# A fused two-layer decoder on one core: constants spread out, the layer change reordered, second-layer steps moved

## The chip, the cores and the metric

The kernel runs on one core of a Trainium2 chip. The core has a matrix engine (TensorE, PE in the profile), a vector engine (VectorE, DVE), a scalar engine (ScalarE, ACT), a general one (GpSimd, POOL) and a queue that only issues transfers (SyncE, SP). ACT and POOL issue transfers too. Engines run their own instructions in order and wait for one another by semaphores. TensorE writes its results to PSUM banks of 128 x 512 numbers; everything else lives in SBUF tiles, or in the chip's main memory (DRAM in the code).

The metric is the device time in microseconds (us) of one execution; lower is better.

## The reference

The input is 512 tokens of 2048 channels, float32, and two residual layers are applied, each `x <- x + W_out(mixer(RMSNorm(x)) * silu(gate))`:

```python
def reference(x, positions, ...):
    hn = rms_norm(x, norm_w[0])                      # layer 0: differential attention, 8 heads
    q, k, v, gate = split(hn @ da_w_in)              # 2048 x 8192
    a = softmax(q1 k1) - lam * softmax(q2 k2)        # causal, RMS-normed and rotated q, k
    x = x + (rms_norm(a @ v) * silu(gate)) @ da_w_out
    hn = rms_norm(x, norm_w[1])                      # layer 1: RWKV-7, 32 heads of 64
    p = token_shift_mix(hn @ rw_w_in, mu)            # r, k, v, gate and two low-rank inputs
    # per head, per token: S = S * w + (S a) b + v k ;  y = S r
    y = group_norm(wkv7_scan(r, w, k, v, -kk, kk * a)) + bonus
    return x + (y * silu(g)) @ rw_w_out
```

The recurrence over tokens is what makes layer 1 more than projections: each head keeps a 64 x 64 state that every token changes.

## The kernel before, in words

Each float32 operand of a large product is split into a high part (a rounded copy, by ACT) and a low part (the rest, by DVE), and three products stand for one (`mm3`). Weights are loaded by SP as `wraw` and split into `wh` and `wl` (`split_w`, L102 and L103), two tiles of each in turn. All large products are recorded under L114.

The order of the work is made in two ways. The instructions are traced in program order, and a planner then orders each engine's instructions by priority as its own estimates of their durations make them ready; `high_priority` with the offsets AHEAD, SCAN and SOLVE (2000, 3000, 4000) lifts a block. Second, a `Chain` is a generator whose pieces of side work are put between matmuls: every matmul of the first `mm3` that carries `g` counts as a tick (`tick`), only the oldest chain counts, and when its wait has run out the next piece is traced, its PE instructions behind that matmul (`issue_after`). The number that a piece yields is the wait to the next. `finish` runs the rest of a chain at once.

**Layer 0.** Per head, two units of 192 matmuls: queries and keys, then values and gate. The attention of head h-1 and the turning of head h's keys run as chains in them. Behind head 0, `rwkv_consts` loads the constants of layer 1 on SP, transposes them on PE (`load_rows`, L187) and derives small tiles on DVE. After the last head, the output projection takes rows that `split_rows` loads back from DRAM and splits (L415, L416); its second half of the columns is done with seven products instead of eight on blocks (`seven`), with sums of row blocks (`sum_forms`, loads `frow`) and of weight blocks.

**Layer change.** The last of the seven products go to the banks `z`. The sums of squares of x are then turned into scales, tokens 0 to 255 first and tokens 256 to 511 after the last product; DVE multiplies x by them (L760), PE transposes it (`xT`, L780), and the low-rank projection (`lora`) begins.

**Layer 1.** Channels go in 16 pairs of heads (j). For each pair there are projections of 48 matmuls: values V(j), keys K(j+1), gate G(j-3) from j = 3 on, receptances R(j+1), in this order. At matmul 18 of V(j) the callback `behind` finishes the chain of pair j-2, computes the Gram matrices of pair j (`gram`, L1004, results `gp`), steps the chain of pair j-1 if it is there, and starts `t_solve` of pair j: a triangular solve on DVE in 31 steps, whose inputs and result T go through DRAM (`ltd`, `LT`, `td`).

The chain of pair j is made at the top of the loop of j+1, and its first step is traced there: four loads of T into `TT` (L1081) and two transpositions on DVE (L1089). After GAP_D ticks the first products with T follow (`px`, L1095), with copies to `X`; after 19 more the second products (L1105) with copies into `TT`; after 8 more the scan, 8 chunks of three steps each (`sm`, L1176, L1187, L1194), with waits of 6, 6 and 8 ticks (4, 4 and 5 for pairs 1 and 14, 3, 3 and 4 for pair 0, whose count is lengthened by 28). Then come the outputs `Y` and `centre` (reductions `s`, L1231 to L1233). `group_norm` (`ysq`, `var`, `rsg`, `yc`) and `finish_y` (four transpositions of `yc`, L1254) end a pair. `px` has one PSUM bank, shared with the values' transpositions, `finish_y` and the sum of `stage_v` that `y` (L1119) reads.

After the loop stand G(13), G(14) and G(15). The chain of pair 15 is put in front of them with a wait of 66 ticks. Between G(14) and G(15) pair 14 is finished. Then rows 0 to 13 are loaded with SP and split, and the output projection follows as in layer 0: two plain column blocks, the second with the sums' loads on POOL's queue, then `seven`. Row 15 comes in the last part of the first column block (`all_rows`). The accumulators `acc` of `seven` use three tiles with the tag AR; the weight loader of `seven` uses tiles with the tags wraw, G1 and LT.

Of the kernel before, what the change touches and what calls it, by code (L numbers as in the profile page):

```python
# [23 lines left out]
P = 128  # L24
# [154 lines left out]

def load_rows(g, pieces, rows, queue=None):  # L180

    nc = g.nc
    t = g.tmpc.tile([P, P], F32, name="prow", tag="junk", bufs=2)
    for r0, n, ap in pieces:
        (queue or nc.sync).dma_start(out=t[r0 : r0 + n, :], in_=ap)
    ps = g.ps.tile([P, 512], F32, name="prp", tag="pc")
    nc.tensor.transpose(ps[:, :rows], t[:rows, :], g.ident[:rows, :rows])  # L187
    o = g.const.tile([P, rows], F32, name=f"prm{pieces[0][2].tensor.name}")
    g.made_prm = nc.vector.tensor_copy(o[:], ps[:, :rows]).ins
    return o  # L190
# [117 lines left out]
def head_vg(g, h, vg):  # L308

    nc, w = g.nc, g.work  # L310
    V = w.tile([P, NT, 256], F32R, name="V", tag="V", bufs=1)
    VL = w.tile([P, NT, 256], F32R, name="VL", tag="VL", bufs=1)
    G = w.tile([P, NT, 256], F32, name="G", tag="G", bufs=1)
    for t in range(NT):
        nc.scalar.activation(V[:, t, :], vg[t][:, 0:256], AF.Copy, scale=g.rstd0[:, t : t + 1])
        nc.vector.scalar_tensor_tensor(VL[:, t, :], vg[t][:, 0:256], g.rstd0[:, t : t + 1], V[:, t, :].bitcast(F32),
                                       ALU.mult, ALU.subtract)
        th = w.tile([P, 256], F32, name="th", tag="th", bufs=2)
        nc.scalar.activation(th[:], vg[t][:, 256:512], AF.Tanh, scale=g.hrstd0[:, t : t + 1])
        gs = w.tile([P, 256], F32, name="gs", tag="gs", bufs=2)  # L320
        nc.vector.scalar_tensor_tensor(gs[:], vg[t][:, 256:512], g.rstd0[:, t : t + 1], g.subw[:],
                                       ALU.mult, ALU.mult)
        nc.vector.scalar_tensor_tensor(G[:, t, :], th[:], 1.0, gs[:], ALU.add, ALU.mult)
    return V, VL, G
# [258 lines left out]
def layer0(g, aps):  # L583
# [86 lines left out]
    with ExitStack() as cx:  # L670
# [186 lines left out]
def rwkv_consts(g, aps):  # L857
# [24 lines left out]
    for nm, first, second in (("bk_s0", "hkk", "hka"), ("bk_b0", "hkk", "omka"),  # L882
# [3 lines left out]
        nc.vector.tensor_copy(o[C:], g.prm[second][C:])  # L886
        g.prm[nm] = o


# [181 lines left out]

GAP_D, GAP_X, GAP_T = 22, 19, 8

# [185 lines left out]
def layer1(g, aps):  # L1259
    nc, tc = g.nc, g.tc  # L1260
    with ExitStack() as cx:
# [97 lines left out]
        acc = {}  # L1359
        for nm in ("11", "22", "12", "21"):  # L1360
            t, c = PLACES[nm]
# [67 lines left out]
```

## Time and profile before

| | us |
|---|---|
| median of 3 runs | 2218.23 |
| lowest, highest | 2218.01, 2223.02 |
| profiled execution | 2227.16 |
| its span, first to last instruction | 2225.5 |
| TensorE busy in it | 2174.8 (98%) |
| VectorE, ScalarE, GpSimd busy | 1425.9, 1041.6, 337.9 |
| TensorE's mean granted clock | 0.994 |

A busy matrix engine is not one at its peak, since matmuls are pipelined. What counts is where it stood still, for what, and where its granted clock was below 1. In rows of waits stand the waiting engine, its result and line, then the one that released it; total in us, number of times, longest. In rows of groups or of the timeline, `out<-in` names the tiles. In the rows of stretches come the stretch, its length, the busy time of each engine with the number of its instructions, the granted clock, and the transfers' share and rate.

### The profile page before, as it was taken

What the parts mean: (1) busy time and instruction counts of PE and PEld (TensorE: products, weight loads), DVE (VectorE), ACT (ScalarE), POOL (GpSimd) and SP (SyncE); (2) the same over time, 40 slices, a digit from 0 to 9 for tenths busy, and PEclk for the clock granted to TensorE, in tenths of its full rate; (3) what the DMA queues carried; (4) which work ended last, traced back from release to release, by engine and by line L of the source; (5) the groups of instructions that cost most, each with busy time, mean ns of one, the idle gap of its engine ahead of it and who ended that gap; (6) DMA issues with size and microseconds to landing.
All of it is one profiled execution on the core that took longest, in us unless ns stands there. A gap on an engine that the chain in (4) does not pass through costs nothing. (4 is left out here: it accounts for less than half of the span.)

```text
span 2225.5 us, 33949 instructions
## 1 busy us (share of the span) xinstructions
PE 2174.8 (98%) x12202; PEld 1761.6 (79%) x12202; DVE 1425.9 (64%) x3772; ACT 1041.6 (47%) x2110; POOL 337.9 (15%) x724
## 2 busy tenths in 40 slices
PE   9999999999999999989999999999999999999999
PEld 7788888888888878867777777877777777777777
DVE  5664636455564676465677787776777877766545
ACT  6443434344343453335455555555555555544322
POOL 0000000000000000110333223323332222331101
PEclk9999999999999999999999999999999999999999
DMA  6223232222222455643423233333333333345465
GB/s 190 91 82 104 76 104 87 92 95 80 95 86 95 141 187 202 158 99 89 106 67 81 75 91 90 79 93 96 90 91 81 90 89 83 102 117 187 151 193 114
DMA packets 281421, 240.21 MB, mean 108 GB/s; under 512 B 31764, under 2 KB 239780, under 8 KB 281252
## 3 DMA queue, kind: packets, MB, share of 16 engines
q1 hardware_dynamic: 257220, 190.22, 29.2%
q0 software_dynamic: 15168, 31.81, 6.8%
q10 hardware_dynamic: 8864, 16.01, 2.0%
q8 instruction: 96, 1.57, 0.3%
q14 instruction: 73, 0.60, 0.1%
HBM read 217.98 MB, written 19.99 MB: 107 GB/s over the span
## 5 line engine op out<-in xcount | busy, mean ns | idle before, releaser
L103 DVE TENSOR_TENSOR wl<-wraw,wh 128x1024 fp32r<-128x1024 f32 (+2 forms) x319 | 388.2, 1217 | 439.7 <-ACT wh L102 431.8
L102 ACT CAST wh<-wraw 128x1024 fp32r<-128x1024 f32 (+2 forms) x319 | 333.5, 1046 | 481.5 <-PE pp L114 342.3
L114 PE MATMUL pp<-wh,hH 128*128 128x512 f32 x1268 | 500.0, 394 | 3.5 <-ACT hH L801 1.5
L114 PE MATMUL pp<-wl,hH 128*128 128x512 f32 x1268 | 496.9, 392 | 1.8 <-DVE wl L103 1.8
L114 PE MATMUL pp<-wh,hL 128*128 128x512 f32 x1268 | 497.9, 393 | 0.0
L114 PE MATMUL pp<-hH,wl 128*128 128x512 f32 x1024 | 416.1, 406 | 0.0
L114 PE MATMUL pp<-hH,wh 128*128 128x512 f32 x1024 | 414.8, 405 | 0.0
L114 PE MATMUL pp<-hL,wh 128*128 128x512 f32 x1024 | 414.3, 405 | 0.0
L114 PEld LDWEIGHTS pp<-wh,hH 128*128 128x128 f32 x1268 | 238.3, 188 | 52.5 <-ACT hH L801 1.8
L114 PEld LDWEIGHTS pp<-wl,hH 128*128 128x128 f32 x1268 | 238.3, 188 | 49.0 <-DVE wl L103 2.5
L114 PEld LDWEIGHTS pp<-wh,hL 128*128 128x128 f32 x1268 | 238.3, 188 | 48.0
L114 PEld LDWEIGHTS pp<-hH,wh 128*128 128x128 f32 x1024 | 194.4, 190 | 34.9 <-issue 1.7
L114 PEld LDWEIGHTS pp<-hL,wh 128*128 128x128 f32 x1024 | 194.3, 190 | 34.9 <-issue 0.2
L114 PEld LDWEIGHTS pp<-hH,wl 128*128 128x128 f32 x1024 | 194.4, 190 | 34.0
L450 POOL DMA_DIRECT2D frow<-yd x12 | 9.0, 748 | 888.0 <-DVE rs_i L63 737.2
L1065 DVE SCALAR_TENSOR_TENSOR tmpl<-LT,Tm 128x60 f32<-128x60 f32 (+24 forms) x496 | 133.7, 270 | 9.9
L1182 POOL COPY SA<-VS 64x64 f32<-64x64 f32 x224 | 55.6, 248 | 504.7 <-DVE VS L1198 424.5
L1067 DVE TENSOR_TENSOR Tm<-Tm,tmpl 128x60 f32<-128x60 f32 (+24 forms) x496 | 104.3, 210 | 11.5
L1179 ACT COPY rhs<-sm 64x64 f32<-64x64 f32 x256 | 52.8, 206 | 88.8 <-PE sm L1176 85.7
L1011 ACT COPY G<-gp 128x512 f32<-128x512 f32 x64 | 35.0, 591 | 90.2 <-PE gp L1004 89.9
L1189 ACT COPY VS<-sm 64x64 f32<-64x64 f32 x256 | 52.6, 206 | 39.9 <-PE sm L1187 35.3
L1187 PEld LDWEIGHTS sm<-rhs,TT 128*128 128x128 f32 x256 | 45.2, 189 | 26.4 <-ACT rhs L1179 18.4
(317 smaller groups left out, 3243.3 us busy)
## 6 DMA issues: line engine op xcount, KB each, us to landing
wraw<-in_rw_w_in_dram SPq DMA_DIRECT2D x128, 512.0 KB, 4.0
wraw<-in_da_w_in_dram SPq DMA_DIRECT2D x254, 256.0 KB, 3.0
wraw<-in_da_w_out_dram SPq DMA_DIRECT2D x26, 512.0 KB, 4.2
wraw<-in_rw_w_out_dram SPq DMA_DIRECT2D x26, 512.0 KB, 4.1
LT<-ltd POOLq DMA_DIRECT2D x64, 132.0 KB, 2.9
yr<-yd SPq DMA_DIRECT2D x28, 256.0 KB, 4.6
frow<-yd POOLq DMA_DIRECT2D x12, 512.0 KB, 5.8
xq<-in_x_dram SPq DMA_DIRECT2D x16, 256.0 KB, 5.5
```

The costliest lines, as they stand in the source:

```text
L102: nc.scalar.copy(hi[:, ks], raw[:, ks])
L103: nc.vector.tensor_sub(lo[:, ks], raw[:, ks], hi[:, ks].bitcast(F32))
L114: m = nc.tensor.matmul(out, a, b, start=s, stop=e, skip_group_check=skip)
L450: nc.gpsimd.dma_start(out=r, in_=src[k0 * P : (k0 + KG) * P, :].rearrange("(k p) t -> p k t", p=P))
L1011: nc.scalar.copy(p.G[:, c0 : c0 + 4, :, h, :], gp[h][:].rearrange("p (u x t) -> p u x t", u=4, x=2))
L1065: nc.vector.scalar_tensor_tensor(tt, LT[:, i : i + 1, i + 1 :].to_broadcast([P, s, n]), n2[:, i : i + 1], Tm[:, 0:s, i : i + 1].to_broadca ...
L1067: nc.vector.tensor_add(Tm[:, 0:s, i + 1 :], Tm[:, 0:s, i + 1 :], tt)
L1179: nc.scalar.copy(rhs[r_, :], sm[r_, h * C : h * C + C])
L1182: nc.gpsimd.tensor_copy(p.SA[r_, c - 1, :], VS[r_, c, h, :])
L1187: nc.tensor.matmul(sm[:, P : P + C], both(g.TT[j % 2][:, c]), rhs[:], start=True, stop=True)
L1189: nc.scalar.copy(VS[r_, c, h, :], sm[r_, P : P + C])
```

## The change

- `load_rows` is divided: `fetch_rows` loads, `load_rows` transposes and copies. `rwkv_consts` becomes a generator. Its loads go to POOL's queue instead of SP's, and its three transpositions and the derived constants become steps of a chain in the first unit of head 1, with waits of 10, 8, 8 and 8 ticks. The PSUM tag of the transpositions is another one. The attention of head 0, which comes behind this chain, waits 24 ticks after it instead of 40.
- `head_vg` keeps its last gate instructions on ACT and DVE; in layer 0, the splits of rows 8 to 13 are put behind them on these engines.
- At the layer change, the scales of tokens 0 to 255 lose the priority SOLVE; those of tokens 256 to 511 keep it.
- GAP_D is 18 instead of 22.
- Pair 14's transpositions, gating and split move from before G(15) to behind its 24th matmul; its gate is computed before them.
- Layer 1's rows are loaded into eight tags instead of four.
- The second and third sums of layer 1 load their rows into G1 tiles instead of LT and BK.
- The accumulators of layer 1 are allocated in the order 11, 21, 22, 12 instead of 11, 22, 12, 21.

```diff
+def fetch_rows(g, pieces, queue, tag="junk", bufs=2):
+    t = g.tmpc.tile([P, P], F32, name="prow", tag=tag, bufs=bufs)
     for r0, n, ap in pieces:
-        (queue or nc.sync).dma_start(out=t[r0 : r0 + n, :], in_=ap)
-    ps = g.ps.tile([P, 512], F32, name="prp", tag="pc")
+        queue.dma_start(out=t[r0 : r0 + n, :], in_=ap)
+    return t
+def load_rows(g, pieces, rows, queue=None, t=None):
+    t = t or fetch_rows(g, pieces, queue)
+    ps = g.ps.tile([P, 512], F32, name="prp", tag="pa", bufs=2)
...
+    g.gated = ta.ins, gd.ins
...
-def split_rows(g, src, tags, bufs, n=KT):
+def split_rows(g, src, tags, bufs, n=KT, late=KT, behind=()):
...
-        out.append(split_row(g, yr[:]))
+        with ExitStack() as after:
+            for ins in behind if k >= late else ():
+                after.enter_context(g.tc.issue_after(ins))
+            out.append(split_row(g, yr[:]))
...
-                Chain(g, attention(g, h - 1, *before, 40 if h < NH - 1 else 36), 40 if h < NH - 1 else 24)
+                Chain(g, attention(g, h - 1, *before, 40 if h < NH - 1 else 36), 40 if 1 < h < NH - 1 else 24)
...
-                rwkv_consts(g, aps)
-        rows = split_rows(g, g.yd, ("t1",), 4, KT - 2)
+                Chain(g, rwkv_consts(g, aps))
+                g.chains[0].step(g)
+        rows = split_rows(g, g.yd, ("t1",), 4, KT - 2, 8, g.gated)
...
-        with tc.high_priority(offset=SOLVE):
-            for half in (slice(0, 2), slice(2, 4)):
+        for half in (slice(0, 2), slice(2, 4)):
+            with tc.high_priority(offset=SOLVE if half.start else 0):
...
-    pb = load_rows(g, [(16 * i, 16, r16(r)) for i, r in enumerate(rows)], 112)
-    g.mu = load_rows(g, [(0, 64, r16(aps["rw_mu"][0, 0 : 4 * D]))], 64)
-    t = g.tmpc.tile([2, RK], F32, name="mut", tag="junk", bufs=2)
-    nc.sync.dma_start(out=t[:], in_=aps["rw_mu"][0, 4 * D :].rearrange("(j p) -> j p", p=RK))
-    ps = g.ps.tile([P, 512], F32, name="pt", tag="pc")
+    tb, tm = [fetch_rows(g, x, nc.gpsimd, "a") for x in (pbs, mus_)]
+    t = g.tmpc.tile([2, RK], F32, name="mut", tag="y", bufs=2)
+    nc.gpsimd.dma_start(out=t[:], in_=aps["rw_mu"][0, 4 * D :].rearrange("(j p) -> j p", p=RK))
+    yield 10
+    pb = load_rows(g, pbs, 112, t=tb)
+    yield 8
+    g.mu = load_rows(g, mus_, 64, t=tm)
+    yield 8
+    ps = g.ps.tile([P, 512], F32, name="pt", tag="pa", bufs=2)
...
+    yield 8
...
-GAP_D, GAP_X, GAP_T = 22, 19, 8
+GAP_D, GAP_X, GAP_T = 18, 19, 8
...
-        finish_y(g, j - 1, pairs[j - 1])
-        row = gated(g, j - 1, pairs[j - 1], gate(g, j - 1, gps), True)
-        gt = gate(g, j, proj(3, j))
-        rows = split_rows(g, g.yd2, ("r", "k", "th0", "th1"), 1, j - 1) + [row]
+        gt = gate(g, j - 1, gps)
+        row = []
+        def last_but_one(m):
+            with tc.issue_after(m.ins):
+                finish_y(g, j - 1, pairs[j - 1])
+                row.append(gated(g, j - 1, pairs[j - 1], gt, True))
+        gt = gate(g, j, proj(3, j, behind=(24, last_but_one)))
+        rows = split_rows(g, g.yd2, ("r", "k", "th0", "th1", "l", "f", "xH", "xL"), 1, j - 1) + row
...
-                frow = [w.tile([P, KG, 512], F32, name="frow", tag=t, bufs=1)[:] for t in ("LT", "BK")]
+                if sums:
+                    both = w.tile([P, 2, KG, 512], F32, name="frow", tag="G1", bufs=2)
+                    frow = [both[:, i] for i in range(2)]
+                else:
+                    frow = [w.tile([P, KG, 512], F32, name="frow", tag=t, bufs=1)[:] for t in ("LT", "BK")]
...
-        for nm in ("11", "22", "12", "21"):
+        for nm in ("11", "21", "22", "12"):
```

More of the change, by code (lines that the diff above doesn't have):

```diff
@@ L177, in unit_tok @@
     return pts
-def load_rows(g, pieces, rows, queue=None):
+def fetch_rows(g, pieces, queue, tag="junk", bufs=2):
+    t = g.tmpc.tile([P, P], F32, name="prow", tag=tag, bufs=bufs)
+    for r0, n, ap in pieces:
+        queue.dma_start(out=t[r0 : r0 + n, :], in_=ap)
+    return t
+def load_rows(g, pieces, rows, queue=None, t=None):
     nc = g.nc
-    t = g.tmpc.tile([P, P], F32, name="prow", tag="junk", bufs=2)
-    for r0, n, ap in pieces:
-        (queue or nc.sync).dma_start(out=t[r0 : r0 + n, :], in_=ap)
-    ps = g.ps.tile([P, 512], F32, name="prp", tag="pc")
+    t = t or fetch_rows(g, pieces, queue)
+    ps = g.ps.tile([P, 512], F32, name="prp", tag="pa", bufs=2)
     nc.tensor.transpose(ps[:, :rows], t[:rows, :], g.ident[:rows, :rows])
@@ L318, in head_vg @@
         th = w.tile([P, 256], F32, name="th", tag="th", bufs=2)
-        nc.scalar.activation(th[:], vg[t][:, 256:512], AF.Tanh, scale=g.hrstd0[:, t : t + 1])
+        ta = nc.scalar.activation(th[:], vg[t][:, 256:512], AF.Tanh, scale=g.hrstd0[:, t : t + 1])
         gs = w.tile([P, 256], F32, name="gs", tag="gs", bufs=2)
@@ L322, in head_vg @@
                                        ALU.mult, ALU.mult)
-        nc.vector.scalar_tensor_tensor(G[:, t, :], th[:], 1.0, gs[:], ALU.add, ALU.mult)
+        gd = nc.vector.scalar_tensor_tensor(G[:, t, :], th[:], 1.0, gs[:], ALU.add, ALU.mult)
+    g.gated = ta.ins, gd.ins
     return V, VL, G
@@ L861, in rwkv_consts @@
             aps["rw_r_k"][0].rearrange("h n -> (h n)"), aps["rw_gn_w"][0], aps["rw_gn_b"][0]]
-    pb = load_rows(g, [(16 * i, 16, r16(r)) for i, r in enumerate(rows)], 112)
-    g.mu = load_rows(g, [(0, 64, r16(aps["rw_mu"][0, 0 : 4 * D]))], 64)
-    t = g.tmpc.tile([2, RK], F32, name="mut", tag="junk", bufs=2)
-    nc.sync.dma_start(out=t[:], in_=aps["rw_mu"][0, 4 * D :].rearrange("(j p) -> j p", p=RK))
-    ps = g.ps.tile([P, 512], F32, name="pt", tag="pc")
+    pbs = [(16 * i, 16, r16(r)) for i, r in enumerate(rows)]
+    mus_ = [(0, 64, r16(aps["rw_mu"][0, 0 : 4 * D]))]
+    tb, tm = [fetch_rows(g, x, nc.gpsimd, "a") for x in (pbs, mus_)]
[7 more added lines that the diff above has]
+    ps = g.ps.tile([P, 512], F32, name="pt", tag="pa", bufs=2)
     nc.tensor.transpose(ps[:RK, :2], t[:], g.ident[:2, :2])
```

## The prediction

> **What bounds the kernel.** I read the page first, then the waits of TensorE (PE), then the clock by stage, then the timeline around the steps that the diff touches.
>
> ```profile
> span 2225.5 us, 33949 instructions
> PE 2174.8 (98%) x12202; PEld 1761.6 (79%) x12202; DVE 1425.9 (64%) x3772; ACT 1041.6 (47%) x2110; POOL 337.9 (15%) x724
> ```
>
> PE is the bound: no edit removes a matmul, so only PE's pauses, and matmuls that run slowly, can be won. The pauses by cause, and what plain products cost back to back in the chain of waits (the last row: start, duration, 19 products, so 0.228 us each):
>
> ```profile
> engine line waited for: us in total, times, longest us
> PE sm L1194 <- ACT VS L1189: 4.3, 15, 1.4
> PE xT L780 <- DVE xq L760: 4.0, 1, 4.0
> PE z L114 <- DVE wl L103: 3.7, 2, 3.4
> PE gp L1004 <- DVE s L1232: 3.2, 8, 0.7
> PE px L1095 <- DVE y L1119: 2.9, 1, 2.9
> PE px L1095 <- DVE T L1089: 2.4, 2, 1.5
> PE pt L1254 <- DVE yc L1247: 2.1, 2, 1.9
> PE pp L114 <- DVE wl L103: 1.8, 2, 1.1
> PE pt L114 <- DVE wl L103: 1.2, 1, 1.2
> PE pp L114 <- ACT hH L415: 0.9, 1, 0.9
> PE pp L114 <- DVE gs L321: 0.7, 1, 0.7
> PE pt L364 <- DVE a L358: 0.7, 1, 0.7
> PE prp L187 <- DVE prmin_rw_w_dram L189: 0.4, 1, 0.4
> PE pp L114 <- DVE prmin_rw_mu_dram L189: 0.3, 1, 0.3
> 1276.27 4.33 PE pp L114 x19
> ```
>
> Some pauses cost twice, because the clock drops behind them:
>
> ```profile
> core 0: us, PE busy (x) PEld busy (x) DVE busy (x) ACT busy (x) POOL busy (x), PEclk, DMA share, GB/s
> 979.00:983.00 4.00, 0.64 (x3) 0.54 (x4) 4.00 (x8) 0.39 (x1) 0.24 (x1) 0.99 0.00 0
> 983.00:986.40 3.40, 3.40 (x10) 2.47 (x9) 0.86 (x2) 0.00 (x0) 0.00 (x0) 0.50 0.41 116
> 1105.80:1109.20 3.40, 1.49 (x34) 1.41 (x35) 1.79 (x4) 1.03 (x2) 3.09 (x5) 1.00 0.92 231
> 1109.20:1116.00 6.80, 6.80 (x47) 5.24 (x46) 1.62 (x3) 3.42 (x7) 0.00 (x0) 0.50 0.13 39
> 2020.60:2024.00 3.40, 1.54 (x10) 1.04 (x9) 1.94 (x5) 1.63 (x2) 0.00 (x0) 1.00 0.55 122
> 2024.00:2027.40 3.40, 3.40 (x10) 2.62 (x9) 2.71 (x4) 0.63 (x1) 0.00 (x0) 0.50 0.32 102
> ```
>
> Each pair of rows is a stretch in which PE did little and the one behind it, at a granted clock of 0.50: 3.4 us at half speed is 1.7 us lost.
>
> **Layer change.** DVE scales the first half of x (eight operations) ahead of a weight split, because the block has priority SOLVE and the split only AHEAD:
>
> ```profile
> 976.01 5.16 DVE L760 TENSOR_SCALAR xq<-xq,rs 128x512 f32<-128x512 f32 x8
> 981.10 1.21 DVE L103 TENSOR_TENSOR wl<-T,wh 128x1024 fp32r<-128x1024 f32 x1
> ```
>
> PE's last products (z) wait 3.4 us for that split. At normal priority the split goes first; the scales follow while the products run. PE then has ten products and DVE only the second split (the ten products of 983.0 to 986.4 needed 0.86 us of DVE), so the scales fit ahead of the transpositions. What is late next is the second half's wait (xT, 4.0 us), which stays. With z's pause the half-speed stretch 983.0 to 986.4 should go. Gain 3.4 + 1.7 = 5.1; if the scales come late after all, 0.
>
> **Last gate.** The transpositions of pair 14 (L1254) stand between two gate projections and wait 1.9 us for its group norm. Moved 24 matmuls into the last projection (24 x 0.228 = 5.5 us), they come after the norm is done. The half-speed stretch 2024.0 to 2027.4 follows that pause: gain 1.9 + 1.7 = 3.6. Row 14 is needed only near the end of the next unit's 192 products.
>
> [...]
>
> **T's products.** GAP_D counts matmuls from the end of the previous chain. Now the scan chain, from the first products on, is 19 + 8 + 7 x (6+6+8) + 6+6 = 179 matmuls, and from matmul 18 of one value projection to the next there are 30 + 3 x 48 = 174. So it ends 5 into the next one, 13 of the 22 are counted at matmul 18, and there gram calls the step itself: first products (px L1095) behind gram, second (L1105) 19 matmuls on. With 18: pair 1's chain (gaps 4 and 5) is 19 + 8 + 7 x 13 + 8 = 126, exactly the 30 + 48 + 48 it has; the count of pair 2 then starts at 0 and expires on matmul 18, ahead of gram, whose own call now issues the second products. From there each chain is 19 ahead, ends 14 before the next value projection, and the pattern repeats: pairs 2 to 14, 13 times. Thus the edit moves 13 scans by 19 matmuls, and the waits of gram for the last scan's reductions (gp <- s, 3.2) vanish: those run about 4 us earlier. The new risk is T itself, which px needs where gram begins now. Pair 4, then pair 12:
>
> ```profile
> 1333.49 0.71 DVE L1231 TENSOR_REDUCE s<-Y 128x4 f32<-128x256 f32 x2
> 1334.13 0.14 DVE L1232 TENSOR_SCALAR s<-s 128x4 f32<-128x4 f32 x1
> 1334.96 0.44 DVE L1089 STREAM_TRANSPOSE T<-TT 64x256 f32<-64x256 f32 x1
> 1334.96 2.71 PE L1004 MATMUL gp<-AR,BK 64*128 64x128 f32 x32
> 1337.59 1.09 PE L1095 MATMUL px<-T,G 32*32 32x32 f32 x32
> 1338.95 0.74 ACT L1098 COPY X<-px 32x256 f32<-32x256 f32 x2
> 1837.51 1.16 PE L1004 MATMUL gp<-AR,BK 64*128 64x128 f32 x16
> 1838.34 0.44 DVE L1089 STREAM_TRANSPOSE T<-TT 64x256 f32<-64x256 f32 x1
> ```
>
> T's second half sits on DVE behind the reductions (0.71 + 0.14 = 0.85), which will be gone by then. Without them T ends at 1335.40 - 0.85 = 1334.55 against gram's 1334.96, 0.4 early, and at 1838.78 - 0.85 = 1837.93 against 1837.51, 0.4 late. Gram itself, and so the next solve, moves back by px's 1.1 us; the group norm that stood ahead of the solve moves forward. I take 0.2 us late per pair, 13 x 0.2 = 2.6, so 3.2 - 2.6 = 0.6. Bounds: never late, 3.2; late by 1.5 each time, the longest wait of px for T in the waits, 3.2 - 19.5 = -16.3. The second products wait for X (ready 1339.69 - 1338.68 = 1.0 after px) behind gram's 2 us: nothing. Pair 0 counts 18 + 28 = 46 instead of 50:
>
> ```profile
> 1106.48 0.44 DVE L1089 STREAM_TRANSPOSE T<-TT 64x256 f32<-64x256 f32 x1
> 1107.71 1.09 PE L1095 MATMUL px<-T,G 32*32 32x32 f32 x32 [2.93 <-DVE y L1119]
> ```
>
> It no longer queues behind y for its bank, but T ends at 1106.92: 0.8 sooner, less 4 products that hid in front (0.9): -0.1. Its half-speed stretch (1109.2 on) stays.
>
> **Tail.** Three waits here rest on transfers (chain of waits):
>
> ```profile
> 2040.81 5.16 DMA yr<-yd
> 2113.61 5.41 DMA frow<-yd
> 2169.49 4.78 DMA acc<-xd
> ```
>
> The row loads have four buffers, and ACT sat on a split whose load was late, with the state copy VS behind it (1.4 at most); eight buffers start the first eight at once and the other six sooner: I take half, 0.7, bounds 0 and 1.4. The sums' loads (frow) shared one pair of buffers, so the third came late and DVE held a weight split behind it: in G1 it need not wait for the second, 1.1. These buffers go to weights later, which queue behind sums that end sooner. The accumulator "21" took the place of "11" after its store, and DVE held a split behind that load: as second it has a free place, 1.2; "12", now fourth, is used only after two more sets of products. Row 15 (hH L415, 0.9): its chain starts 23 matmuls earlier (5.2 us), 0.9. Sum 3.9.
>
> **First layer.** The constants' transpositions stood at the end of a unit: 0.4 + 0.3 go; the next split's 0.7 (of the 1.8) may stay, as the small DVE operations now have priority SCAN. Gain 0.7, bounds 0 and 1.4. Their loads leave SP for POOL, which has nothing to do in that part. Attention of head 0 starts 18 matmuls later, and a step of keys more falls at its unit's end: nothing, PE has products to put between. Row splits from row 8 on go behind the last gate on ACT and DVE: the waits for gs and for a, 0.7 each, are DVE behind row splits; the splits are needed later, rows 8 on only after 96 products (22 us). I take 0.7 of 1.4.
>
> **Sum.** 5.1 + 3.6 + 0.6 - 0.1 + 3.9 + 0.7 + 0.7 = 14.5. The profiled execution took 2227.16 (its span 2225.5), so 2212.7; against the median of the runs, 2218.23, which lies 8.9 lower, 2203.7.
>
> **The rivals.** 0.3% is 6.7 us, about what a measurement of this kernel tells from no change.
> (a) T's products late, slower than before. For: in the two pairs whose px already is placed as soon as the order allows, it waited for T (2.4 in 2, longest 1.5), so the planned order counts T too early. Against: in pair 4 it would be early. At 1.5 each the term is -16.3 instead of 0.6, and the low stretch of pause and 32x32 products resembles 1105.8 to 1109.2, behind which the clock halved: 1.7 in half of 13 pairs, 11. 14.5 - 16.9 - 11 = -13.4: 2232. It decides from 1.3 per pair (13.9 of other gains + 3.2, over 13), 1.8 for a slowdown of 0.3%, less if the clock falls.
> (b) T late by 0.9: 3.2 - 11.7 = -8.5, total 5.4, 2213: the loop gives the rest back.
> (c) The edit does not do what it says: the planner sees T too late and gives PE to gram first; px stays behind it and the second products, now without their 19, wait 1.0 for X: 3.2 - 13 = -9.8, total 4.1, 2214. For: gram is ready then. Against: T is done within 0.4 of it.
> (d) The pauses go, but not the clock's or the layer change's gain (scales late): 14.5 - 3.4 or - 5.1, 2207 to 2209.
> (e) The half-speed stretch of pair 0 (6.8 us, 3.4 lost) and a like one at pair 2 fall away too, as every later pause shifts: 2197.
>
> **How the numbers follow.** Forecast 0.45, own range 2199 to 2209 (constants, row splits and row loads 0.7 each, T 2.6, all up or all down); (d) 0.17, (e) 0.05, (b) 0.12, (c) 0.08, (a) 0.13. Faster: 0.45 + 0.17 + 0.05 = 0.67; same 0.20; slower 0.13. The range 2197 to 2221 leaves out (a) and some of (e).
>
> **What would show it.** z without a pause and full clock before the layer change's one remaining wait; no half clock in the last gates; px ahead of gram in pairs 2 to 14 with waits for T under 0.4; no gp wait for s; no splits held by frow or acc. Wrong, if px waits for T for over a microsecond in most pairs, or half-speed stretches appear between them.

## The result, and the profile after

| | before | changed | ratio, with its 95% interval |
|---|---|---|---|
| median (lowest to highest), us | 2220.61 (2218.01 to 2223.02) | 2208.17 (2203.95 to 2213.33) | 0.9944, 0.9928 to 0.9961 |
| a second comparison | 2227.44 (2221.68 to 2229.04) | 2208.02 (2207.30 to 2208.98) | 0.9915, 0.9902 to 0.9928 |
| profiled execution | 2227.16 | 2213.33 | |
| its span | 2225.5 | 2211.6 | |

The change is faster, by 12.4 us in one comparison and 19.4 in the other; 14.5 were forecast. The profiled execution before is 4 us slower than all six runs of the first row and lies among those of the second, so differences between single traces hold only as far as other traces confirm them. The sum is right and several of its parts are not. These are TensorE's waits in the changed kernel (waiting engine, result and line, what released it; total us, times, longest):

```profile
engine line waited for: us in total, times, longest us
PE px L1112 <- DVE T L1106: 7.4, 10, 2.4
PE xT L790 <- DVE xq L770: 5.0, 1, 5.0
PE sm L1211 <- ACT VS L1206: 4.2, 16, 0.7
PE sm L1193 <- DVE VS L1215: 3.6, 15, 0.5
PE pp L114 <- ACT hH L421: 2.4, 1, 2.4
...
PE sm L1204 <- ACT rhs L1196: 0.6, 2, 0.3
```

Gone are z (3.4), gp for s (3.2), the pause of 1.9 us at row 14's transpositions and the three waits for wl in constants (0.7) and tail (1.1 and 1.2). Also gone, and in no term of the forecast, is most of sm for rhs: 5.3 us in the trace before, 0.6 now. New are T's waits and one of 2.4 us for the first split row of the output projection (hH, L421). The granted clock has new stretches at 0.50 too. Windows of the changed kernel (stretch, its length, busy time of each engine with instructions, PEclk, DMA share, GB/s):

```profile
core 0: us, PE busy (x) PEld busy (x) DVE busy (x) ACT busy (x) POOL busy (x), PEclk, DMA share, GB/s
981.74:988.57 6.83, 3.55 (x10) 2.10 (x11) 6.30 (x22) 1.27 (x2) 0.00 (x0) 0.50 0.10 31
1097.79:1111.45 13.66, 13.48 (x88) 10.54 (x89) 3.02 (x5) 5.28 (x12) 3.17 (x5) 0.50 0.32 81
1387.93:1391.34 3.41, 2.67 (x52) 2.19 (x52) 2.95 (x5) 1.61 (x4) 0.00 (x0) 1.00 0.67 171
1391.34:1398.17 6.83, 6.83 (x61) 5.56 (x58) 0.69 (x1) 4.58 (x10) 2.61 (x5) 0.50 0.09 12
...
1766.81:1773.63 6.82, 6.82 (x56) 5.45 (x55) 0.69 (x1) 4.78 (x10) 3.05 (x6) 0.50 0.08 10
2026.22:2029.63 3.41, 1.01 (x7) 0.53 (x5) 2.42 (x3) 3.36 (x7) 0.00 (x0) 1.00 0.00 0
2029.63:2033.05 3.42, 3.42 (x11) 2.77 (x10) 2.65 (x5) 3.38 (x8) 0.00 (x0) 0.50 0.68 219
```

Pair 0's stretch has doubled to 13.7 us, pairs 5 and 11 (1391, 1767) have one each, and the last gate's has moved from 2024 to 2030, behind the new wait of 2.4 us.

**The stages of all fourteen traces.** The large products with 512 moving columns (projections, `lora`, output projections) are the same number in every kernel, 7704. Counted in order of their starts, they cut each trace into stages: the starts of products 432, 3072, 3840, 4224, 4512, 6816 and 7152 are read from the trace, and the differences stand below. C holds the first layer's output projection and the layer change, G pair 15, the last gates and the first rows of the output projection, H the rest.

| us | A: to 432 | B: 3072 | C: 3840 | D: pair 0 | E: pairs 1, 2 | F: pairs 3 to 14 | G: to 7152 | H: to the end | span |
|---|---|---|---|---|---|---|---|---|---|
| before | 118.6 | 682.8 | 204.6 | 112.6 | 114.5 | 756.4 | 101.7 | 134.2 | 2225.5 |
| layer change alone | 121.8 | 683.8 | 201.0 | 112.3 | 113.5 | 754.6 | 98.7 | 142.1 | 2227.7 |
| tail alone | 118.2 | 682.7 | 204.8 | 112.1 | 113.3 | 755.4 | 102.7 | 130.7 | 2220.0 |
| T at 18 alone | 121.4 | 682.7 | 203.0 | 115.6 | 112.8 | 749.6 | 93.9 | 132.7 | 2211.6 |
| changed | 116.4 | 682.3 | 199.7 | 115.5 | 112.5 | 756.2 | 98.4 | 130.6 | 2211.6 |
| changed, second trace | 116.4 | 682.7 | 199.8 | 115.5 | 111.0 | 751.0 | 98.6 | 130.7 | 2205.6 |
| layer change undone | 118.3 | 682.6 | 206.1 | 114.2 | 111.0 | 748.4 | 99.5 | 130.6 | 2210.7 |
| last gate undone | 118.4 | 683.5 | 201.1 | 114.2 | 111.1 | 750.0 | 94.6 | 130.6 | 2203.4 |
| row 14 at 12 | 118.1 | 683.6 | 201.0 | 114.0 | 111.0 | 752.7 | 95.3 | 130.6 | 2206.4 |
| rows 0 to 13 first | 118.4 | 682.2 | 200.1 | 114.2 | 111.2 | 748.5 | 96.3 | 130.7 | 2201.5 |
| T back at 22 | 117.0 | 682.3 | 199.7 | 112.1 | 111.6 | 753.1 | 97.5 | 130.8 | 2204.0 |
| T at 22, row 14 at 12 | 118.3 | 682.1 | 200.3 | 112.4 | 110.3 | 753.7 | 98.5 | 130.7 | 2206.2 |
| three edits together | 116.2 | 682.5 | 199.9 | 112.2 | 111.4 | 759.8 | 97.5 | 130.6 | 2210.0 |
| 8 matmuls behind gram | 116.8 | 683.5 | 201.1 | 116.5 | 111.8 | 764.0 | 97.2 | 130.6 | 2221.5 |

Much of what differs within a stage is time at half speed: in the changed kernel's trace products of 512 columns start 0.427 us apart at 0.50 (1395.58 to 1397.72) and 0.227 at full clock (1386.67 to 1387.80). With half the length of its stretches at 0.50 taken off, C is 199.3 to 199.7 in the four traces with the old order at the layer change and 195.9 to 197.6 in the ten with the new; D is 108.6 to 109.2 in all but the last row (111.4), E 109.9 to 111.8 in all, and F 748.4 to 750.0 in the seven with T at 18 whose chain is otherwise unaltered. H needs no correction to show the tail's edit: 130.6 to 130.8 in the eleven traces that have it.

### The profile page after: what moved, and what is told of

Its sections match the earlier page's. It is cut to its first block, busy times and chain, and to the rows that moved or that the text cites. A ratio compares the mean times of both kernels' runs of the same rounds, so it can differ in the third digit from the quotient of the medians.

```text
span 2211.6 us, 33922 instructions
## 1 busy us (share of the span) xinstructions
PE 2173.2 (98%) x12202; PEld 1762.5 (80%) x12202; DVE 1445.7 (65%) x3772; ACT 1040.9 (47%) x2110; POOL 359.8 (16%) x733
## 5 line engine op out<-in xcount | busy, mean ns | idle before, releaser
L1082 DVE SCALAR_TENSOR_TENSOR tmpl<-LT,Tm 128x60 f32<-128x60 f32 (+24 forms) x496 | 133.1, 268 | 10.6
L1199 POOL COPY SA<-VS 64x64 f32<-64x64 f32 x224 | 61.2, 273 | 428.2 <-DVE VS L1215 382.9
L1215 DVE SCALAR_TENSOR_TENSOR VS<-sm,gam,Sg 64x64 f32<-64x64 f32 x192 | 54.2, 282 | 50.9 <-PE sm L1211 46.5
L1202 POOL TENSOR_SCALAR Sg<-SA,gam 128x64 f32<-128x64 f32 x96 | 72.9, 759 | 9.3
```

The costliest lines, as they stand in the source:

```text
L1082: nc.vector.scalar_tensor_tensor(tt, LT[:, i : i + 1, i + 1 :].to_broadcast([P, s, n]), n2[:, i : i + 1], Tm[:, 0:s, i : i + 1].to_broadca ...
L1199: nc.gpsimd.tensor_copy(p.SA[r_, c - 1, :], VS[r_, c, h, :])
L1202: nc.gpsimd.tensor_scalar(Sg[:], p.SA[:, c - 1, :], p.gam[:, c : c + 1], None, ALU.mult)
L1215: g.state = nc.vector.scalar_tensor_tensor(VS[r_, c + 1, h, :], s_, p.gam[r_, c : c + 1], Sg[r_, :], ALU.mult, ALU.add)
```

## The experiments

Theory A: T's products at 18 gain some 1 us in an undisturbed pair, but T then comes late and the small products stand together (px, gram, px2 without a matmul between them), so that half-speed stretches appear in some pairs and eat the gain. Its rivals: the move is worth about 1 us per pair net, or about nothing, as forecast. Theory B: the 2.4 us wait for hH comes from rows 0 to 13 being split behind row 14 on ScalarE; its rival: their loads or tiles bound it. Beside these, the layer change, the tail and the last gate were tried alone or undone; the constants and the splits of rows 8 to 13 were not.

**T back at 22**

```diff
-GAP_D, GAP_X, GAP_T = 18, 19, 8
+GAP_D, GAP_X, GAP_T = 22, 19, 8
```

> The changed kernel with the distance of T's products put back from 18 to 22 matmuls of the chain, and nothing else. Theory A (what moving T's products up gains per undisturbed pair, about 0.6 to 1.2 us in the comparison of the two traces, is spent again in pairs where T's transposes come late and a half-speed stretch of 6.8 us follows, in pairs 5 and 11 of the changed kernel's trace at about 3.4 us each): the ten waits of px for T (7.4 us) and the half-speed stretches of pairs 5 and 11 go, the waits of the score tile for s (gp, 3.2 us) return, and the time is the changed kernel's within 3 us, 2205 to 2211. Rival (the move is worth about 1 us in each of 13 pairs net, the stretches come from elsewhere): 6 to 10 us more than the changed kernel, 2214 to 2218, with half-speed stretches in the pairs as often as there.

2205.71 us, 0.9915 of before (0.9901 to 0.9929): by the time, undoing the move of T's products costs nothing against the changed kernel (0.9944 and 0.9915), as theory A expected. TensorE's waits in this kernel:

```profile
PE sm L1204 <- ACT rhs L1196: 5.6, 15, 0.5
...
PE px L1112 <- DVE T L1106: 2.4, 2, 1.5
PE gp L1021 <- DVE s L1249: 2.4, 5, 0.8
```

The waits for rhs and s are back, eight of the ten for T are gone, no stretch at half speed is left in pairs 3 to 14, and pair 0's is 6.8 us long again. Against the changed kernel's second trace it loses 2.0 in F and wins 3.4 in D and 1.1 in G. So gain and loss do cancel as theory A has it, but against that trace the loss is mostly in pair 0 and the last gates, not in stretches of the pairs behind.

**T at 18 alone, on the kernel before**

```diff
-GAP_D, GAP_X, GAP_T = 22, 19, 8
+GAP_D, GAP_X, GAP_T = 18, 19, 8
```

> The kernel before with T's products at 18 instead of 22 alone. From the comparison of the traces of before and of the changed kernel's second execution, pairs 3 to 14 gain 9 us (the waits of gp for s, 3.2 us in all, and of sm for rhs, 0.38 us in each of some 12 pairs, go, and smaller ones), pair 0's longer half-speed stretch takes 3 us back, and stretches of 3.4 us in chance pairs 1.7 to 3.4 us more: 3 to 6 us less than the kernel before, 0.997 to 0.9985. Rival (moving T's products 18 matmuls on gives nothing without the rest of the change, as the prediction's 0.6 us said): 0.999 to 1.001.

2213.59 us, 0.9938 (0.9924 to 0.9953): 12.8 us, two to four times the 3 to 6 expected, and the rival, with the forecast's 0.6, is refuted. The stages of the trace say where: D +2.9, F -6.8, G -7.8. The others (A +2.9, C -1.6, E -1.7, H -1.4) are not put down to this edit: in C and E a stretch at half speed of 3.4 us is missing or shorter, and A has one more; H's part is open. For F, the waits of TensorE between the same products (pairs 3 to 14), first before, then with this edit alone:

```profile
PE sm L1187 <- ACT rhs L1179: 4.8, 12, 0.7
PE gp L1004 <- DVE s L1232: 3.2, 8, 0.7
PE sm L1194 <- ACT VS L1189: 2.7, 13, 0.6
```

```profile
PE sm L1194 <- ACT VS L1189: 3.3, 14, 0.4
PE sm L1176 <- DVE VS L1198: 2.5, 12, 0.5
PE px L1095 <- DVE T L1089: 1.7, 5, 0.5
PE sm L1187 <- ACT rhs L1179: 0.6, 2, 0.3
```

10.7 us become 8.1. The other part is inside gram. In the timeline of this run, pair 4's gram (start, duration) takes 2.06 us where the forecast's rows have 2.71:

```profile
1335.74 0.69 PE L1095 MATMUL px<-T,G 32*32 32x32 f32 x16
1336.71 0.69 PE L1095 MATMUL px<-T,G 32*32 32x32 f32 x16 [0.28 <-DVE T L1089]
1337.43 2.06 PE L1004 MATMUL gp<-AR,BK 64*128 64x128 f32 x32
1339.41 1.09 PE L1105 MATMUL px<-TT,X 32*32 32x32 f32 x32
```

From the first to the last start, gram takes 1.78 us in all twelve pairs here; before, it takes 2.36 to 3.26 in ten of them. Over twelve pairs that is 21.4 against 32.0 us; 3.2 of the 10.6 us between them are the listed waits; the rest are products of its second half that start late or no longer two by two. Against it, px stretches: 1.66 us from the first start here (the first two rows), where the forecast's row has 1.09. For G, the last step of pair 14's group norm (yc; first and last start at the end), before and with this edit:

```profile
L1247 DVE TENSOR_TENSOR yc<-yc,rsg x1: 691/691/691, 2022.2 to 2022.2; 128x512 f32<-128x512 f32 x1
```

```profile
L1247 DVE TENSOR_TENSOR yc<-yc,rsg x1: 693/693/693, 2013.9 to 2013.9; 128x512 f32<-128x512 f32 x1
L1254 PE MATMUL pt<-ident,yc x4: 270/272/272, 2014.9 to 2015.2; 128*128 128x128 f32 x4
```

The earlier chain brings the norm forward: row 14's transpositions no longer wait, though they stand where they stood before. The pause that the last gate's edit is for goes without that edit.

**Last gate undone**

```diff
-        gt = gate(g, j - 1, gps)
...
-        gt = gate(g, j, proj(3, j, behind=(24, last_but_one)))
+        finish_y(g, j - 1, pairs[j - 1])
+        row = [gated(g, j - 1, pairs[j - 1], gate(g, j - 1, gps), True)]
+        gt = gate(g, j, proj(3, j))
```

> The changed kernel with the last pair but one finished ahead of the last gate's projection, as in the kernel before. The prediction's second step (finishing it inside the gate saves 1.9 us of pause and 1.7 us of half speed): 3.6 us more than the changed kernel. Theory B (the gain was given back by the 2.4 us wait at the first out-projection and the half speed behind it): the pause of 1.9 us at the transposes of row 14 returns, the wait at the first out-projection goes, and the time is the changed kernel's within 1.5 us, 0.991 to 0.993 of the kernel before.

2204.65 us, 0.9900 (0.9883 to 0.9916). Neither expectation held: no pause returns, the wait for hH is gone, and G is 3.8 to 4.0 us shorter than in the changed kernel's two traces. From its trace, the norm, then the splits of rows 0 to 13 and of row 14:

```profile
L1264 DVE TENSOR_TENSOR yc<-yc,rsg x1: 693/693/693, 2007.0 to 2007.0; 128x512 f32<-128x512 f32 x1
...
L421 ACT CAST hH<-yr x14: 604/617/622, 2016.8 to 2027.8; 128x512 fp32r<-128x512 f32 x14
L421 ACT CAST hH<-mixv x1: 614/614/614, 2016.2 to 2016.2; 128x512 fp32r<-128x512 f32 x1
```

In the changed kernel's second trace the norm is done as early, and everything behind it is late:

```profile
L1264 DVE TENSOR_TENSOR yc<-yc,rsg x1: 693/693/693, 2005.2 to 2005.2; 128x512 f32<-128x512 f32 x1
...
L1271 PE MATMUL pt<-ident,yc x4: 272/272/273, 2017.8 to 2018.1; 128*128 128x128 f32 x4
...
L421 ACT CAST hH<-yr x14: 601/616/622, 2022.2 to 2034.8; 128x512 fp32r<-128x512 f32 x14
L421 ACT CAST hH<-mixv x1: 621/621/621, 2020.0 to 2020.0; 128x512 fp32r<-128x512 f32 x1
```

The transpositions start 12 us behind the end of the norm, row 14 is split at 2020.0, and rows 0 to 13 come behind it.

**Row 14 at 12 matmuls, and rows 0 to 13 first**

```diff
-        gt = gate(g, j, proj(3, j, behind=(24, last_but_one)))
+        gt = gate(g, j, proj(3, j, behind=(12, last_but_one)))
```

> The changed kernel with the last pair but one finished 12 matmuls into the last gate's projection instead of 24. [...] Rival (the row loads or the release of their tiles bound the first split, wherever row 14 stands): the wait stays at 2 to 2.5 us and the time stays at 2208.

2205.60 us, 0.9914 (0.9896 to 0.9932). Twelve of the gate's products are 2.7 us (they start 0.227 us apart in the changed kernel's trace). The wait for hH and the stretch behind it are gone, and G is 95.3 against 98.4 and 98.6; a wait of 0.8 us of px for y appears instead. The second way:

```diff
+        rows = split_rows(g, g.yd2, ("r", "k", "th0", "th1", "l", "f", "xH", "xL"), 1, j - 1)
         gt = gate(g, j, proj(3, j, behind=(24, last_but_one)))
-        rows = split_rows(g, g.yd2, ("r", "k", "th0", "th1", "l", "f", "xH", "xL"), 1, j - 1) + row
+        rows = rows + row
```

> The changed kernel with the splits of rows 0 to 13 put ahead of the last gate's projection in the program, so that they take the hH tiles and ScalarE ahead of row 14's split. Theory B (the 2.4 us wait at the first out-projection is that queueing): row 0 is split some 2 us or more sooner, the wait falls under 0.5 us, the half-speed stretch at 2030 us goes, and the time is 2.4 to 4 us less than the changed kernel's. Rival (the loads of the rows or the release of a tile by an earlier reader bound it): the wait stays at 2 us or more, and the time is the changed kernel's; a second rival, that the rows' splits now stand ahead of the gate's own work on ScalarE, puts a wait of 0.5 us or more into the last gate.

2204.78 us, 0.9901 (0.9889 to 0.9914), 3.2 us less than the changed kernel on the same chip, its slowest run below the fastest there. The splits start at 2006.0, row 14's is at 2023.2, and the last gates run at full clock with 0.27 us of pause in 16:

```profile
2014.00:2030.00 16.00, 15.73 (x103) 12.64 (x102) 12.29 (x19) 10.39 (x22) 1.74 (x3) 1.00 0.53 177
```

Theory B holds in both: the loads did not bind the first row, its place behind row 14's split did. Both edits move the rows on ScalarE and in the hH tiles at once, so which of the two queues held them is not parted.

**T at 22 and row 14 at 12**

> The changed kernel with T's products back at 22 and the last pair but one finished 12 matmuls into the last gate instead of 24. In the run with 22 alone the wait at the first out-projection was gone already (row 14 was split at 2016.8 us, 2.3 us ahead of the gate's last product), so if theory B is right there is little left to gain: within 1.5 us of that run, 0.990 to 0.993 of the kernel before, 3 to 7 us less than the changed kernel. Rival (the two edits' gains of about 2.5 us each add up): 0.988 to 0.990 of the kernel before. A second rival: the transposes of row 14, now 12 matmuls sooner, wait for its y and a pause of 0.8 us or more opens in the last gate.

2209.56 us, 0.9922 (0.9910 to 0.9934), on the chip where the changed kernel has 0.9915: the two edits do not add up, and the second rival's pause is there. With T at 22 the wait for hH was gone already; 12 matmuls bring waits of 0.8 for yc and 1.1 for mixv instead, and G is 1.0 longer than with 24.

**The changed kernel once more**

> The changed kernel once more, unaltered, beside the next three on the same chip. If the half-speed stretches of pairs 5 and 11 depend on where the 3.4 us windows happen to fall against the late T's, another execution has them in other pairs or in fewer, while the waits of px for T and the 2.4 us wait at the first out-projection stand again; time 0.993 to 0.996 of the kernel before. Rival: the same stretches in the same pairs.

0.9915, as in the table, a little less than the 0.993 to 0.996 expected. The waits are those of the first trace; the stretches at half speed in pairs 5 and 11 are not there. Pair 3 has one instead, of 3.4 us, and pair 5 runs at full clock:

```profile
1265.42:1268.84 3.42, 3.42 (x39) 3.20 (x37) 0.33 (x1) 2.38 (x5) 0.00 (x0) 0.50 0.21 62
1391.00:1398.00 7.00, 7.00 (x85) 6.04 (x85) 2.14 (x3) 6.37 (x14) 3.31 (x6) 1.00 0.23 56
```

Of the seven traces with T at 18 in this order, four have no such stretch in pairs 3 to 14 (F 748.4 to 750.0, mean 749.1), and the others have 3.4 us of it (751.0), 6.8 (752.7) and twice 6.8 (756.2). With T at 22, five traces have none and F is 753.1 to 756.4, mean 754.6. So the move gains 5.5 us in these pairs, and each 6.8 us at half speed takes about 3.5 back. The first trace of the changed kernel, the slowest of its six runs, is the unlucky one.

**Eight matmuls behind gram**

```diff
-GAP_D, GAP_X, GAP_T = 18, 19, 8
+GAP_D, GAP_X, GAP_T = 18, 8, 8
...
-                    gram(g, j, p, j > 1 and pairs[j - 1].chain)
+                    gram(g, j, p, j == 2 and pairs[j - 1].chain)
```

> The changed kernel with eight matmuls of the chain between the Gram products and the second set of T's products (px, gram, eight, px2), where the changed kernel has px, gram and px2 back to back. Theory A (the half-speed stretches in the pairs follow a 3.4 us window in which a late T and the run of small products leave few columns moving): the small products no longer stand together, no half-speed stretch is left in pairs 3 to 14 though the waits of px for T stay, and the time falls by 3 to 7 us against the changed kernel, to 2201 to 2205. Rival (the wait for T itself brings the stretch, or which pair has one is chance): stretches of 6.8 us in two or so pairs as before and 2208 within 2 us; a second rival, that the second set of products or the copies behind them come due too late, gives waits of the chain's steps of 0.5 us or more in each of 12 pairs and 2212 or more.

2224.60 us, 0.9999 (0.9987 to 1.0010), the second rival. Three stretches of 3.4 us at half speed are in F all the same, and the steps of the scan wait in every pair:

```profile
PE sm L1211 <- ACT VS L1206: 9.4, 14, 0.9
PE sm L1193 <- DVE VS L1215: 7.0, 16, 0.7
```

Parting the small products thus neither removes the stretches nor is free; it says nothing on whether their standing together brings the stretches, since T's waits grew too (7.4 to 11.8 us).

**The layer change alone, and undone**

```diff
-        with tc.high_priority(offset=SOLVE):
-            for half in (slice(0, 2), slice(2, 4)):
+        for half in (slice(0, 2), slice(2, 4)):
+            with tc.high_priority(offset=SOLVE if half.start else 0):
```

> The kernel before with the layer change's reordering alone (the second half's scaling and products at their own place instead of ahead of all). The theory of the prediction's first step: the 3.4 us wait for z and most of the half-speed stretch at 983 us go, 5 us less than the kernel before, about 2215. Rival (the scaling of the second half now comes late and the wait of the products xT for xq grows by as much, or the half-speed stretch only moves): no change within 1.5 us of the kernel before.

2223.24 us, 0.9991 (0.9977 to 1.0006): no difference. The profiled execution was the slowest of the twelve (2229.38; the others from 2215.11), so its trace cannot say why the median gains nothing. In it the wait for z is gone and C is 3.6 us shorter, but H is 8.0 longer. The rows of accumulators in the timeline of DVE, first before, then with this edit:

```profile
2174.39 1.28 DVE L514 TENSOR_TENSOR acc<-acc,pt 128x512 f32<-128x512 f32 x2 [2.46 <-DMA acc<-xd]
```

```profile
2174.05 1.28 DVE L514 TENSOR_TENSOR acc<-acc,pt 128x512 f32<-128x512 f32 x2 [6.78 <-DMA acc<-xd]
```

The transfer that the tail's edit takes out of the way kept DVE waiting 4.3 us longer here: from issue to landing it took 8.5 us (2165.45 to 2173.93) instead of 4.8 (2169.49 to 2174.27). TensorE waited 4.4 for that, and a half-speed stretch of 6.8 us followed. Why the transfer took longer is open. The edit's worth is seen where the tail is mended, by taking it out of the changed kernel (the diff above, reversed):

> The changed kernel with the layer change put back to its order before (both halves' scaling ahead of all), and nothing else. Alone on the kernel before, this edit gave 3.6 us at the layer change in the trace and nothing in the time, because a late load of the last rows cost 4.4 us in the tail of the profiled execution. Theory: the 3.6 to 5 us are real wherever nothing behind them gives them back, so without the edit the wait of z returns at 3.4 us and the time is 3.5 to 5 us more than the changed kernel's. Rival (the layer change's gain is given back by later work whatever the tail does, as in the run with that edit alone): the changed kernel's time within 1.5 us.

2214.89 us, 0.9948 (0.9935 to 0.9961), 6.9 us more than the changed kernel on the same chip, where 3.5 to 5 were expected; C is 6.3 longer than in that kernel's second trace, with z's wait back at 3.5 and 13.7 us at half speed instead of 6.8. The theory holds against its rival: the layer change's gain is real in the changed kernel.

**The tail alone**

```diff
-        rows = split_rows(g, g.yd2, ("r", "k", "th0", "th1"), 1, j - 1) + [row]
+        rows = split_rows(g, g.yd2, ("r", "k", "th0", "th1", "l", "f", "xH", "xL"), 1, j - 1) + [row]
...
+                    both = w.tile([P, 2, KG, 512], F32, name="frow", tag="G1", bufs=2)
...
-        for nm in ("11", "22", "12", "21"):
+        for nm in ("11", "21", "22", "12"):
```

> The kernel before with the tail's three edits alone: the last rows' buffers in two copies, the order of the accumulations 11, 21, 22, 12, and eight row buffers instead of four. The prediction's fifth step: the waits of wl (1.1 and 1.2 us), of hH (0.9 us) and of the last sums (0.7 us) go, 3.5 to 5 us less than the kernel before, 0.9977 to 0.9985. Rival (the waits are hidden by the last sums and stores anyway, or come back at the next product): 1 us less at most, 0.9995 or more.

2222.27 us, 0.9977 (0.9966 to 0.9988): 4.1 us by the medians, as expected. H is 3.5 shorter; the tail's two waits for wl are gone. The wait for hH in the tail (0.9) stays, and G is no shorter.

**Three edits together**

```diff
-    for h in range(2):
-        for half in range(2):
+    for half in range(2):
+        for h in range(2):
...
-    yield GAP_D
+    yield GAP_D if j else 22
```

with the rows 0 to 13 first, as above.

> The changed kernel with three edits: the splits of rows 0 to 13 ahead of the last gate's projection (3.2 us by the medians of the last runs), T's products of pair 0 alone back at 22 matmuls (the half-speed stretch of pair 0 was 6.8 us long with 22 and 10.2 to 13.7 us with 18), and T's four loads by halves, so that the first products' two loads go first. If the three add up: pair 0's stretch at 6.8 us, the five waits of 0.4 us for T in pairs 3 to 14 gone, 5 to 8 us less than the changed kernel, 0.987 to 0.989 of the kernel before. If only the rows count: 0.990.

2210.26 us, 0.9922 (0.9904 to 0.9939), where the rows alone had 0.9901 on another chip. Pair 0 came out as hoped (D 112.2), but F is 759.8, 10.7 above the 749.1 of the traces without half speed. 8.5 of these are half the length of two stretches at 0.50, in pairs 3 and 9. Beside them TensorE waits for AR, which gram needs and which now stands behind the late transposition of T on DVE. Gram waits for AR once, for 1.1 us, where T's loads are in the old order, with pair 0 at 22 as well (T back at 22), so the loads by halves are the likely cause. The stretches, TensorE's waits, and DVE's timeline in pair 5:

```profile
1262.27:1272.51 10.24, 9.60 (x74) 8.13 (x75) 2.03 (x3) 6.27 (x12) 2.66 (x5) 0.50 0.15 34
1641.15:1647.98 6.83, 6.83 (x59) 5.56 (x56) 0.69 (x1) 4.35 (x9) 2.73 (x5) 0.50 0.09 12
```

```profile
PE gp L1021 <- DVE AR L1005: 7.2, 12, 1.1
...
PE px L1112 <- DVE T L1106: 4.1, 6, 1.5
```

```profile
1389.58 0.44 DVE L1106 STREAM_TRANSPOSE T<-TT 64x256 f32<-64x256 f32 x1 [0.30 <-DMA TT<-td]
1390.06 0.75 DVE L854 SCALAR_TENSOR_TENSOR mixr<-pp,prmin_rw_mu_dram,mixr 128x511 f32<-128x511 f32 x1
1390.84 0.69 DVE L1005 TENSOR_TENSOR AR<-mixr,E 128x512 f32<-128x512 f32 x1
```

The waits for T in pairs 3 to 14 are not gone (1.7 us in four places, 2.3 in seven in the changed kernel's second trace), and a new wait, for the next thing on the same engine, came beside them (6.1 of the 7.2 us in these pairs).

The best versions run are the changed kernel with the rows first (0.9901, faster than the changed kernel's 0.9915 on the same chip) and with the last gate undone (0.9900 on another chip; its interval, 0.9883 to 0.9916, overlaps the changed kernel's, so only stage G of the traces shows that gain). Pair 0 alone back at 22 with the loads left as they are was not tried.

## Why the prediction was right, and where it was not

- **Layer change, 5.1: right, a little large.** The four traces with the old order (before, tail alone, T at 18 alone, undone) have 204.6 in C on average, the ten with the new one 200.4: 4.3, of which 3.1 remain when half speed is taken off. z's wait of 3.4 went as forecast, and the wait that was to stay, xT, grew from 4.0 to 5.0. The stretch at half speed behind z's pause went in the changed kernel (10.2 us in all became 6.8), but that gain is less sure than the forecast had it: two of the ten traces with the new order have 10.2 too, and of the four with the old order one has 6.8 and one 13.7.
- **Last gate, 3.6: the step that failed.** With T at 22 its reasoning may be right: G is 97.5 and 98.5 with the edit, 98.7 to 102.7 without it. But T at 18 brings the norm 3.7 us forward within G (28.9 us behind its start against 32.6) and removes the pause by itself (G 93.9 on the kernel before), and then the edit only delays row 14, and behind it rows 0 to 13: it costs 3.9 (98.5 against 94.6). "Row 14 is needed only near the end of the next unit's 192 products" was true of row 14 and missed what queues behind its split on ScalarE.
- **T's products, 0.6: the mechanism was right, the size wrong.** px stands ahead of gram in pairs 2 to 14, the waits for s are gone, and T is late by 0.1 to 0.2 us per pair in F by the listed waits (1.7 in the run alone, 2.3 in the second trace), by 0.3 if all is counted that px takes longer; 0.2 per pair were taken. What the sum left out: the waits for rhs (4.8 to 0.6 us), whose rows stood in the waits but not in the prediction, and gram's own slow second half (7.4 beside the 3.2); against them stand 3.1 more of waits for the scan's VS and some 3.8 that px takes longer, T's waits between its products in it. With the 3.2 for s that comes to 7.9 in the run alone, where F fell by 6.8; without stretches it is 5.5 on average, and 3.7 as a mean over all seven traces (750.9 against 754.6). Another 7.8 came in G, which the last gate's edit then gave back in part.
- **Pair 0, -0.1: wrong.** D is 114.7 on average with 18 and 112.3 with 22. The prediction let the half-speed stretch stay; it grew from 6.8 us to 10.2 or 13.7, which is 1.7 to 3.4 lost and, by the stages without half speed, the whole of the loss.
- **Tail, 3.9: the sum right, the parts in part.** H is 3.5 shorter than before, and every trace with the edit has 130.6 to 130.8, where those without it have 132.7, 134.2 and 142.1. So `frow` and the accumulators gave 2 us or more, for which 2.3 were taken; the eight row buffers' 0.7 cannot be found in G (102.7 with the tail alone). The hH wait's 0.9 did go with the earlier chain, as forecast: it stays with the tail alone and with T at 22 (0.9 in both).
- **First layer, 1.4.** A is 2.1 shorter between the first traces. Executions differ by some us in the arrival of the first operands (product 48 starts at 20.9 to 21.6 us, or at 22.6 to 24.6), but from there to product 432 the ten traces with the edit take 95.3 to 95.4 us and three of the others 97.1 or 97.2 (T at 18 alone 98.8, with 3.4 us at half speed): 1.8, more than the 0.7 for the constants and outside its bound of 1.4. The waits of 0.4 and 0.3 went, and the next split's 0.7 as well; the rest of the 1.8 is not explained. The row splits' 0.7 was hardly there: the waits for gs and a behind them, 1.4 before, are 0.9 in the first trace of the changed kernel and 2.0 with the last gate undone.
- **Pairs 1 and 2** became 1 to 4 us shorter, in runs with T at 22 as well. Most of it is the stretch at half speed of pair 2: 6.8 us in the trace before, 3.4 or none in the others; without half speed E is 111.1 before and 109.9 to 111.8 in the rest. Only rival (e) speaks of it, and nothing shows that an edit did it.
- **The rivals.** (a) named the right place, a stretch of waits and 32x32 products with the clock at 0.50 behind it (pair 5's, 1387.93 and 1391.34 above), and charged it to half of 13 pairs; in pairs 3 to 14 it came in none to two. (e)'s stretch at pair 2 did go in the changed kernel's second trace, but pair 0's grew. Of the signs named in advance, half-speed stretches between the pairs, a sign of being wrong, did come, and the last gates' half clock did not go. The waits went as said, but for T's: up to 0.6 us in pairs 3 to 14 of the first trace and 1.4 in the pairs ahead of them, where less than 0.4 was forecast.

By stages, the gain forecast and the gain in the changed kernel's two traces against before's:

| us | A | B | C | D | E | F | G | H | sum |
|---|---|---|---|---|---|---|---|---|---|
| forecast | 0.7 | 0 | 5.8 | -0.1 | 0 | 0.6 | 5.2 | 2.3 | 14.5 |
| first trace | 2.1 | 0.5 | 4.9 | -2.8 | 2.0 | 0.2 | 3.3 | 3.5 | 13.8 |
| second trace | 2.2 | 0.1 | 4.8 | -2.9 | 3.6 | 5.4 | 3.2 | 3.5 | 19.9 |

(Forecast: C holds the layer change and the row splits, G the gate and 0.7 and 0.9 of the tail, H the other 2.3.) That the total came so near is partly luck: what was missed in A, E, F and H outweighs what was lost in D and G, and in the first trace two stretches at half speed took F's gain again.

On the half-speed stretches, the first row of pair 5 in the windows above has TensorE busy for 2.67 of 3.41 us, and the clock was 0.50 in the 6.8 us behind it. In the last gate before, it was busy for 1.54 of 3.40 us (2020.60), and the clock was 0.50 in the 3.4 us behind.

## What to carry to other kernels

Where two edits of one change work on the same wait, price each with the other in place: here an earlier chain removed the pause that the second edit was for, and the second edit then cost 3.9 us. Price a group of products by its own first-to-last time as well as by the list of waits: pair 4's gram, 2.71 us in the quoted rows, took 2.06 with the edit, and over twelve pairs only 3.2 of 10.6 us stood in the list. And compare several traces stage by stage, because which pairs fell into half speed changed here from one trace to the next, by up to 7 us in all (F, 756.2 against a mean of 749.1).

## What the runs showed of the hardware

- Stretches of 3.41 us at full clock that the clock of 0.50 followed had TensorE busy for 1.01 us (2026.22 in the changed kernel; 3.42 us at 0.50 behind it), for 2.67 in pair 5 (1387.93; 6.83 behind it) and, in 3.42 us, for 2.65 in pair 11 (1763.39; 6.82 behind it). In the second trace of the same kernel pair 5 ran at 1.00 (1391.00 to 1398.00).
- In the timeline of the changed kernel, the stretch of pair 5 ahead of the half speed has 32 products of 32 columns, 18 of 128 and the ends of two of 512: some 3,350 columns (an estimate, with a product that crosses a border shared out by its modelled time). At 0.228 us for 512 columns, plain products move some 7,700 in 3.41 us (an estimate). So TensorE was busy for 78% of that stretch and moved under half of those columns, as theory A has it in the run with eight matmuls behind gram; that few columns bring the half speed is not shown by it.
- The stretches at half speed in pair 0 were 13.66 and 13.65 us long in the changed kernel's two traces, 10.24 with rows 0 to 13 first, an edit outside pair 0, and 6.83 with T back at 22.
- One transfer of the residual rows took 4.8 us from issue to landing in one execution and 8.5 in another, in two kernels whose tails are the same, and held DVE for 2.46 and 6.78 us.
